# FF2 as seven products of quadrants, in a transformer layer on one core

## The chip, the cores and the metric

The kernel runs on one core of a Trainium2 chip. The time is the device time of one execution in microseconds; a run gives one time, and the median of several runs stands for a kernel. The profiled execution is one more run, with the hardware profiler on; its trace has every instruction.

Engines are called as in the profile: PE multiplies matrices (PEld loads its stationary operand), DVE and ACT work on tiles element by element, POOL does so too and issues DMAs, SP only issues DMAs.

## The reference

One layer: a token mixer (attention with a window, and a gated delta rule), a projection w_out, a layer norm, and an MLP with squared ReLU and a second norm. Sequence 1024, width 1024, hidden width 4096, float32. The part that the change touches is the end:

```python
mixed = (sigmoid(g_a) * y_a + sigmoid(g_b) * y_b) @ w_out
x = layer_norm(ALPHA * x + (1.0 + gt1) * mixed, ln1_g, ln1_b)
u2 = x * (1.0 + sc2) + sh2
h = square(relu(u2 @ w_ff1 + b_ff1))                              # FF1
x = layer_norm(ALPHA * x + (1.0 + gt2) * (h @ w_ff2 + b_ff2), ln2_g, ln2_b)   # FF2
```

## The kernel before

**Splits.** Each float32 operand is taken as a sum of two parts. ACT copies it into the high part, DVE subtracts that from the operand and has the low part (`split_s`, L215 and L216; "hi" and "lo" below). A product is three matmuls: hi·hi, hi·lo, lo·hi. The moving side is 512 columns wide.

**Seven products.** w_out's input and FF1 go by Strassen's scheme in Winograd's form: operands are cut into quadrants, sums of quadrants are formed, and seven products of halves replace eight.

**The order.** PE, DVE and ACT run in an order written out by the program: `at(p, f)` puts the instructions of `f` at matmul number p, counted from the start, and a matmul of 512 columns is one slot of it. `E0`, `F0` and `G0` are the slots at which w_out, FF1 and FF2 begin. The queues of SP (DMA) and of POOL (arithmetic and DMA) are ordered by a scheduler, and each runs in its order.

**w_out** (L1485): 4 segments of 96 matmuls. A segment is one half of the columns (`q`) and four of the eight token tiles; four weights of a segment are loaded and split. `mix_done` adds the residual and, when both halves are there, normalises the tile; `u2_done` then transposes it on PE (L1408), ACT writes the pieces to `rawu` (L1411), and the quadrants and sums are split (u11, u21, u22 and the sums' `mh`, `ml`).

**FF1** (L1805): 1344 matmuls, 16 pairs of hidden blocks, 7 products of 12 for each. A pair holds blocks 2i and 2i+1; POOL forms the sums of its weights (`f_sums`, `f_sums2`), `f_alpha`, `f_beta`, `f_gamma`, `f_delta` split them. The first 5 pairs (`EARLY`) are interleaved, since the second half of the tokens comes later; the other 11, here called dense, follow one after the other, 84 slots each. The results, four blocks of a pair, are squared and stored to DRAM (`hid_d`).

**FF2** (L1873): 1536 matmuls in six chunks over the hidden width, of 2, 6, 6, 6, 6 and 6 blocks; the weights of a chunk stay, the hidden blocks are loaded tile by tile and split, and each chunk's result is added to `acc` from PSUM (L1834). The residual is added tile by tile in the last chunk but one (`residual`), and in the last each tile is normalised (`norm2`) while PE works on the next.

Of the kernel before, what the change touches and what calls it, by code (L numbers as in the profile page):

```python
# [34 lines left out]
def hybrid_layer_kernel(ctx: ExitStack, tc: tile.TileContext,  # L35
# [42 lines left out]
    r_d = dram.tile([NT, P, D], F32, name="r_d")  # L78
    gt_d = dram.tile([2, D], F32, name="gt_d")
    res_d = dram.tile([NT, P, D], F32, name="res_d")  # L80
    hid_d = dram.tile([NT, P, D_FF // P, P], F32, name="hid_d")
# [83 lines left out]
    wseq += [in_cols(w_ff1, 2 * i * P) for i in range(EARLY - 1)]  # L165
# [1191 lines left out]
    def open_pe():  # L1357
# [5 lines left out]
        gt1 = pe.tile([P, D], F32, name="gt1", bufs=1)  # L1363
# [11 lines left out]
    xqs, rs = {}, {}  # L1375

    def x_load(q, t):
        xq = xqs[q, t] = pe.tile([P, HALF], F32, tag="xq", name="xq", bufs=4)
        nc.sync.dma_start(out=xq, in_=x[t * P:(t + 1) * P, halves[q]])

    def mix_done(q, t, pt):
        if q == 0:
            rs[t] = pe.tile([P, D], F32, tag="r", name="r", bufs=4)
        r = rs[t]
        rq = r[:, halves[q]]
        V.tensor_tensor(out=rq, in0=pt, in1=gt1[:, halves[q]], op=ALU.mult)
        V.scalar_tensor_tensor(out=rq, in0=xqs.pop((q, t)), scalar=ALPHA, in1=rq, op0=ALU.mult, op1=ALU.add)
        V.bn_stats(out=parts[:, t, q, :], in_=rq)
        if q == 0:
            return  # L1390
# [82 lines left out]
    for s in range(4):  # L1473
        for t in range(4):
            p = E0 + SEG * s + 48 * (t // 2)
            at(max(E0 + 15, p - 40), x_load, s % 2, 4 * (s // 2) + t)
    wt, bank = [], 0

# [11 lines left out]
    for s in range(4):  # L1490
        base, q, t0 = E0 + SEG * s, s % 2, 4 * (s // 2)
        del wt[:]
        groups = [[[0, 1], [2, 3]], [[0, 1], [2, 3]], [[4], [5, 6, 7]], [[4], [5], [6], [7]]][s]
        free = [(0, 0, 60, 72), (0, 0, 60, 72), (0, 0, 42, 60), (0, 0, 78, 84)][s]
        for ts in groups:
# [5 lines left out]
            for c in range(4):  # L1501
                if len(wt) == c:
                    wt.append(stream_w(max(0, base + free[c] - count[0]), 1))
                for pt, t in zip(pts, ts):
                    mix_mm(pt, slice(t * P, (t + 1) * P), c)
            for pt, t in zip(pts, ts):
                at(max(count[0] + 1, E0 + 28), mix_done, q, t, pt)
                if q == 1:
                    at(count[0] + 1, u2_done, t, count[0] + (34 if len(ts) == 2 else 24))

    assert count[0] == F0
    pf = pf_pool = None
    WF, ring, fraw, tls = {}, [0], {}, {}

    def ring_tiles(shape):
        n = ring[0]
        ring[0] += 1
        if n % 6 < 4:  # L1520
            pool, th, tl, bufs = wp, "wh", "wl", 4
        elif n < 6:
            pool, th, tl, bufs = pf, "fh", "fl", 2
        else:
            pool, th, tl, bufs = big2, f"h{2 + n % 6}", f"l{2 + n % 6}", 1
        return (pool.tile(shape, F32R, tag=th, name="wfh", bufs=bufs), pool.tile(shape, F32R, tag=tl, name="wfl", bufs=bufs))

    def w_split(name, src):
        WF[name] = hi, lo = ring_tiles([P, KT, P])
        split_s(hi, lo, src, 5)  # L1530

    def f_raw(i, j):
        raw = wp.tile([P, KT, P], F32, tag="wr", name="fraw", bufs=2) if i == 0 or (i, j) == (EARLY - 1, 2) else \
            pf.tile([P, KT, P], F32, tag=("fh", "fl")[j], name="fraw")
        nc.sync.dma_start(out=raw, in_=in_cols(w_ff1, (2 * i + j % 2) * P)[0])
        fraw.setdefault(i, {})[j] = raw

    def f_load(i):

        for j in range(2):  # L1540
            f_raw(i, j)

    def f_sums(i, E):

        f1, f2 = fraw[i][0], fraw[i][1]
        X = fraw[i]["x"] = pf.tile([P, 4, P], F32, tag="x", name="x", bufs=1)
        sub(E, X, f1[:, 0:4, :], f2[:, 0:4, :])
        E.tensor_tensor(out=f2[:, 0:4, :], in0=f2[:, 0:4, :], in1=f2[:, 4:8, :], op=ALU.add)
# [7 lines left out]
    def f_alpha(i, j=0):  # L1556
        w_split((i, "a"), fraw[i][j])
# [12 lines left out]
    def open_pf():  # L1570
        nonlocal pf, pf_pool
        pe_pool.__exit__(None, None, None)
        pf_pool = tc.tile_pool(name="pf", bufs=2, side="right")
        pf = pf_pool.__enter__()

    def tile_of(i, c):
        t = tls[i, c] = pf.tile([P, HALF], F32, tag="t", name="t", bufs=6)
        return t

    def bias(i, c):  # L1580
        f = 2 * i + c // 2
        return bf1[:, f:f + 1]

# [4 lines left out]
    def out_block(i, c):  # L1588
        t = tls.pop((i, c))
        f, h = 2 * i + c // 2, c % 2  # L1590
        nc.sync.dma_start(out=hid_d[4 * h:4 * h + 4, :, f, :].rearrange("t p c -> p t c"), in_=t.rearrange("p (t c) -> p t c", t=4))

    def full(i, c, pt):
        t = tls[i, c]
        V.tensor_tensor(out=t, in0=t, in1=pt, op=ALU.add)
        if i < EARLY and c == 0:
            after(3, square, i, c)
            return
        V.scalar_tensor_tensor(out=t, in0=t, scalar=0.0, in1=t, op0=ALU.max, op1=ALU.mult)
        out_block(i, c)  # L1600

    def square(i, c):
# [3 lines left out]
        out_block(i, c)  # L1606

    def last_block(i, c, pt):
# [3 lines left out]
        out_block(i, c)  # L1612
# [11 lines left out]
    OPEN_PF = F0 + 46  # L1624
# [7 lines left out]
    at(OPEN_PF, open_pf)  # L1632
    ring[0] = EARLY - 1
    at(F0 + 15, f_raw, EARLY - 1, 2)
    at(OPEN_PF + 6, f_alpha, EARLY - 1, 2)
    at(F0 + 42, f_raw, 0, 1)
    at(OPEN_PF + 16, f_raw, 0, 0)
    at(F0 + 84, f_sums, 0, V)
    at(F0 + 85, f_sums2, 0, V)
    at(F0 + 96, f_gamma, 0)  # L1640
    at(F0 + 104, f_beta, 0)
    at(pos[0, 5] + 10, f_delta, 0)
    for i in range(1, NPAIR):
        if i < EARLY:
            b = pos[i, 5]
            E = V if i == 1 else G
            at(b - (47 if i == 1 else 70), f_load, i)
# [5 lines left out]
        else:  # L1653
            b = pos[i, 1]
            d = 36 if i == EARLY else 0
            at(b - 104, f_load, i)
            at(b - 84, f_alpha, i)
            at(b - 84 + d, f_sums, i, G)
            at(b - 76 + d, f_sums2, i, G)
            at(b - 58 + d, f_beta, i)  # L1660
            at(b - 38 + d, f_gamma, i)
            at(max(b - 22 + d, pos[i - 1, 7] + 13), f_delta, i)


    chunks = [(0, 2)] + [(2 + 6 * c, 6) for c in range(5)]
    NCH = len(chunks)
    starts = [G0 + 2 * NT * 3 * f for f, _ in chunks]
    W2, hid, acc, rows_, rr = {}, {}, [None] * NT, {}, {}
    p2f = p2f_pool = None

    def w2_tiles(f):

        if f < 2:
            return ring_tiles([P, D])
        g = (f - 2) % 6
        if (f - 2) // 6 % 2 == 0:
            at_ = (big2, f"h{g}"), (big2, f"l{g}")
        else:
            at_ = ((big, f"l{2 * g}"), (big, f"l{2 * g + 1}")) if g < 4 else ((big2, f"h{2 + g}"), (big2, f"l{2 + g}"))
        return [pool.tile([P, D], F32R, tag=tag, name="w2") for pool, tag in at_]  # L1680

    def w2_load(f, raw):
        W2[f, "raw"] = raw
        nc.sync.dma_start(out=raw, in_=w_ff2[f * P:(f + 1) * P, :])

    def w2_split(f):
        raw = W2[f, "raw"]
        if f >= chunks[-1][0]:

            V.tensor_tensor(out=raw, in0=raw, in1=rows_["gt2"], op=ALU.mult)  # L1690
        W2[f] = hi, lo = w2_tiles(f)
        split_s(hi, lo, raw, 5)

    def hid_load0(m, raw):

        hid["raw", m] = raw.rearrange("p (t f c) -> p t f c", t=4, f=2)
        nc.sync.dma_start(out=hid["raw", m], in_=hid_d[4 * m:4 * m + 4, :, 0:2, :].rearrange("t p f c -> p t f c"))

    def hid_split0(m):
        hi, lo = ring_tiles([P, 4, 2, P])  # L1700
        split_s(hi, lo, hid["raw", m], 5)
        for i in range(4):
            hid[0, 4 * m + i] = hi[:, i], lo[:, i]

    units = [(c, t) for c in range(1, NCH) for t in range(NT)]

    def hid_tile(kind, n, dtype):
        return big.tile([P, 6, P], dtype, tag=f"h{2 * kind + n % 2}", name="hid")

    def hid_load(n):  # L1710
        c, t = units[n]
        hid["raw", n] = hid_tile(0, n, F32)
        nc.sync.dma_start(out=hid["raw", n], in_=hid_d[t, :, chunks[c][0]:chunks[c][0] + 6, :])

    def hid_split(n):
        hid[units[n]] = hi, lo = hid_tile(1, n, F32R), hid_tile(2, n, F32R)
        split_s(hi, lo, hid.pop(("raw", n)), 5)

    def open_p2f():
        nonlocal p2f, p2f_pool  # L1720
        pf_pool.__exit__(None, None, None)
        p2f_pool = tc.tile_pool(name="p2f", bufs=2, side="right")
        p2f = p2f_pool.__enter__()

# [12 lines left out]
    def rr_tile(t):  # L1737
        rr[t] = big.tile([P, D], F32, tag=f"h{6 + t % 2}", name="rr")
        nc.sync.dma_start(out=rr[t], in_=res_d[SLOTS[t]])

    def res_sums(t, i):

# [3 lines left out]
        else:  # L1746
            V.tensor_tensor(out=r, in0=r, in1=rows_["B2"], op=ALU.add)
            nc.sync.dma_start(out=res_d[SLOTS[t]], in_=r)

    def residual(t, i):  # L1750
        if i == 0:
# [161 lines left out]
```

## Time and profile before

| | us |
|---|---|
| median of 3 runs | 1919.66 (1917.45 to 1919.95) |
| the profiled execution | 1921.89 |
| its span | 1920.2 |
| w_out, 1143.00 to 1246.15 | 103.15 |
| FF1, 1246.15 to 1560.98 | 314.83 |
| FF2, 1560.98 to the last matmul | 351.37 |
| tail | 7.85 |

The stages follow one another on PE, so each can be read on its own; what comes before w_out stays as it is. A row of a timeline gives the start, the duration, engine, line and operation, the tiles written and read, their shapes, and in brackets the idle time of the engine ahead of it with what ended it. A row of groups gives, behind the bar, the busy time and the mean duration in ns, then idle time. A row of waits gives the waiting instruction, what it waited for, the total, the number and the longest.

### The profile page before, as it was taken

The numbers are of one execution on the slowest core, as the hardware profiler recorded it, in microseconds if no ns is written. First come the engines' busy times: TensorE is split into PE (matmuls) and PEld (weight loads), VectorE is DVE, ScalarE is ACT, GpSimd is POOL, SyncE is SP. The second block draws the span as 40 slices with busy tenths as digits, with TensorE's granted clock in tenths as the row PEclk, the third lists the DMA queues.
The fourth block names the chain that finished last, engine by engine and source line by source line (L and its number), as shares of the span: only waits on it lengthen the run. The fifth ranks groups of instructions, "written<-read, shape, count | busy, mean of one in ns | idle before, by whom it ended". The sixth has DMA issues, their size and how long they took to land.

```text
span 1920.2 us, 25900 instructions
## 1 busy us (share of the span) xinstructions
PE 1867.6 (97%) x9323; PEld 1542.8 (80%) x9323; DVE 1223.5 (64%) x2347; ACT 882.3 (46%) x1985; POOL 353.4 (18%) x437
## 2 busy tenths in 40 slices
PE   7999999999999999999999999989999999999998
PEld 5977788788887878888888887768888878888887
DVE  7678598898855666666644447774545435444677
ACT  3689666666654445554634223563333342211110
POOL 7333223433331000000001100004323200000000
PEclk8999999999999999999999999999999999999999
DMA  9655632232258444554347445245434355444422
GB/s 255 180 186 199 208 91 82 62 95 79 68 198 218 146 137 145 155 154 139 111 132 257 146 132 199 100 133 158 121 110 115 109 174 197 152 143 143 135 95 82
DMA packets 255273, 275.56 MB, mean 144 GB/s; under 512 B 23477, under 2 KB 202630, under 8 KB 254890
## 3 DMA queue, kind: packets, MB, share of 16 engines
q1 hardware_dynamic: 233802, 199.05, 34.7%
q0 software_dynamic: 21344, 74.88, 11.8%
q8 instruction: 73, 1.20, 0.2%
q14 instruction: 54, 0.44, 0.1%
HBM read 194.44 MB, written 77.34 MB: 142 GB/s over the span
## 4 chain that ended last, share of the span: by engine, by line
PE 79%; DVE 7%; ACT 4%; DMA 3%; issue 2%; POOL 0%; SPq 0%; ACTq 0%; POOLq 0%; DVEq 0%
PE mm L248 31%; PE mm L1805 8%; PE a L1873 6%; PE mm L1873 6%; PE b L1873 6%; PE b L1805 4%; PE a L1805 2%; PE mm L1485 2%; PE c L909 2%; DVE wl L216 1%; PE a L1485 1%; PE mm L188 1%; PE mm L187 1%; PE mm L186 1%; PE a L1167 1%
## 5 line engine op out<-in xcount | busy, mean ns | idle before, releaser
L248 PE MATMUL mm<-uh,wl 128*128 128x512 f32 x800 | 332.0, 415 | 0.0
L248 PE MATMUL mm<-ul,wh 128*128 128x512 f32 x800 | 321.2, 402 | 0.0
L248 PE MATMUL mm<-uh,wh 128*128 128x512 f32 x800 | 318.0, 398 | 0.0
L248 PEld LDWEIGHTS mm<-ul,wh 128*128 128x128 f32 x800 | 151.0, 189 | 26.7 <-issue 0.2
L248 PEld LDWEIGHTS mm<-uh,wl 128*128 128x128 f32 x800 | 151.6, 189 | 23.0 <-issue 3.9
L248 PEld LDWEIGHTS mm<-uh,wh 128*128 128x128 f32 x800 | 151.6, 189 | 21.3 <-issue 0.2
L215 ACT ACTIVATE hid<-hid 128x768 fp32r<-128x768 f32 x40 | 33.8, 845 | 177.5 <-PE a L1873 60.1
L1873 PE MATMUL a<-w,hid 128*128 128x512 f32 x486 | 115.0, 390 | 0.3 <-DVE hid L216 0.3
L1873 PE MATMUL mm<-w,hid 128*128 128x512 f32 (+1 forms) x486 | 112.6, 385 | 0.0
L1873 PE MATMUL b<-w,hid 128*128 128x512 f32 (+1 forms) x486 | 112.6, 385 | 0.0
L1873 PEld LDWEIGHTS a<-w,hid 128*128 128x128 f32 x486 | 91.1, 188 | 19.8 <-DVE hid L216 0.7
L216 DVE TENSOR_TENSOR wl<-wr,wh 128x1024 fp32r<-128x1024 f32 x84 | 102.2, 1219 | 6.4 <-ACT wh L215 6.4
L1873 PEld LDWEIGHTS b<-w,hid 128*128 128x128 f32 x486 | 90.1, 188 | 18.3
L1873 PEld LDWEIGHTS mm<-w,hid 128*128 128x128 f32 x486 | 90.1, 188 | 18.2
L215 ACT ACTIVATE wh<-wr 128x1024 fp32r<-128x1024 f32 x84 | 88.1, 1049 | 19.8 <-PE c L1485 12.3
L216 DVE TENSOR_TENSOR wfl<-fraw,wfh 128x1024 fp32r<-128x1024 f32 x44 | 64.2, 1460 | 45.0 <-ACT wfh L215 44.9
L842 DVE CUSTOM_DVE_ANT_0 nscore<-a,amask,nsink 128x256 f32<-128x256 f32 (+1 forms) x128 | 54.6, 464 | 34.3 <-PE a L835 33.5
L853 POOL TENSOR_TENSOR sm<-sm 128x256 f32<-128x256 f32 x56 | 55.6, 994 | 98.6 <-ACT sm L849 65.8
L1169 ACT ACTIVATE vn<-a,brk 128x128 f32<-128x128 f32 x64 | 23.5, 367 | 108.2 <-PE a L1167 107.4
L849 ACT ACTIVATE sm<-nscore,stat 128x257 f32<-128x257 f32 (+1 forms) x128 | 62.1, 488 | 4.1 <-DVE stat L842 3.6
L894 POOL TENSOR_SCALAR_AFFINE_SELECT pl<-ph 128x512 fp32r<-128x512 f32 x56 | 44.0, 786 | 90.4 <-DVE ph L887 71.7
L737 DVE TENSOR_TENSOR M<-M,stt 128x62 f32<-128x62 f32 (+30 forms) x62 | 57.8, 933 | 1.5
(544 smaller groups left out, 4621.9 us busy)
## 6 DMA issues: line engine op xcount, KB each, us to landing
wr<-in_w_in_dram SPq DMA_DIRECT2D x60, 512.0 KB, 3.7
fraw<-in_w_ff_dram SPq DMA_DIRECT2D x33, 512.0 KB, 4.2
hid_d<-t SPq DMA_DIRECT2D x64, 256.0 KB, 2.3
w2raw<-in_w_ff_dram SPq DMA_DIRECT2D x32, 512.0 KB, 3.4
hid<-hid_d SPq DMA_DIRECT2D x40, 384.0 KB, 3.3
adaw<-in_w_ada_dram SPq DMA_DIRECT2D x41, 256.0 KB, 2.7
adaw<-in_w_ada_dram SPq DMA_DIRECT2D x16, 512.0 KB, 6.4
wr<-in_w_out_dram SPq DMA_DIRECT2D x16, 512.0 KB, 3.8
```

Of the source, the lines that this page charges most:

```text
L215: A.activation(out=hi, in_=src, func=AF.Copy)
L216: after(lag, lambda: V.tensor_tensor(out=lo, in0=src, in1=hi.bitcast(F32), op=ALU.subtract))
L248: T.matmul(ts[half], lhsT=w[:, k, :], rhs=xx[k][:, sl], start=k == 0 and m == 0, stop=k == KT - 1 and m == 2)
L737: V.tensor_tensor(out=M[:, 0:s, s + 1:64], in0=M[:, 0:s, s + 1:64], in1=steps.pop(s), op=ALU.add)
L842: V.tensor_tensor_reduce(out=ns[:, i, 1:1 + W], in0=sc[:, i * 2 * P:i * 2 * P + W], in1=amask[:, mo:mo + W], scale=-1.0, scalar=nsink[:, 2 ...
L849: A.activation(out=sm[:, i, 0:1 + W], in_=ns[:, i, 0:1 + W], func=AF.Exp, scale=-1.0, bias=st[:, i:i + 1], accum_out=st[:, 2 + i:3 + i])
L853: G.tensor_tensor(out=sm[:, :, 1 + P:1 + 2 * P], in0=sm[:, :, 1:1 + P], in1=sm[:, :, 1 + P:1 + 2 * P], op=ALU.add)
L894: G.affine_select(out=flat4(part), in_=flat4(full), pattern=[[0, 4], [1 if odd else -1, P]], compare_op=ALU.is_ge if odd else ALU.is_gt, f ...
L909: T.matmul(av[:, 0:256], lhsT=vt[:, b, :], rhs=p_[:, m, :], start=p_ is full and m == 0, stop=p_ is prods[-1][1] and m == 1)
L1485: T.matmul(pt, lhsT=m[k][:, tok], rhs=w[:, k % 2, :], start=k == 0 and w is wh and m is mh, stop=k == KT - 1 and m is ml)
L1805: T.matmul(pt, lhsT=a[:, k0 + k, :], rhs=b[k], start=begin and k == 0 and x_ == 0, stop=k == 3 and x_ == 2, skip_group_check=True)
L1873: T.matmul(pt, lhsT=a[:, j, :], rhs=b[:, lo:up], start=j == 0 and x_ == 0, stop=j == n - 1 and x_ == 2)
```

## The change

**FF2** becomes seven products too. The hidden activations are cut into quadrants, half of the tokens by half of the hidden width (16 blocks), and w_ff2 likewise. The products run in the order 1, 2, 6, 5, 7, 3, 4; each has 8 steps of 24 matmuls, 1344 in all. A step loads one hidden piece (128 x 2 x 512, from `hf_d`) and one weight piece (from w_ff2, or for the products 4 to 7 from `wt_d`) and splits both. Results of a chain of products stay in PSUM and are added on; `take` copies or adds them to `acc`. The last three steps of the last product (`LAST`) run token tile by token tile. Gates, residuals and norms of all tiles stand in and behind the last product (`gated`, `norm2`).

**FF1** pairs block i with i+16, so that a pair has one block of each half. It stores three of its blocks and the four sums of blocks that FF2 needs (`h_sums`, `h_sums2`, on DVE). For the first five pairs a block is loaded back once (`again`).

**Weight sums:** for each pair of rows of w_ff2, `t_load` loads two tiles (SP), `t_make` forms four sums on POOL and stores the tiles to `wt_d` from POOL's queue. Fifteen of the sixteen rounds are placed in FF1 and use the one pair of tiles h6 and l6.

**w_out** takes the column halves in the order 0, 1, 1, 0, so that the third segment uses the second's weights; twelve weights are loaded instead of sixteen. The tokens' x is loaded as whole rows, and tiles 4 and 5 are finished together.

```diff
+    hf_d = dram.tile([7, D_FF // (2 * P), P, HALF], F32, name="hf_d")
+    wt_d = dram.tile([D_FF // (2 * P), 2, P, D], F32, name="wt_d")
...
-    for q in (0, 1, 0, 1):
+    for q in (0, 1, 0):
...
-        groups = [[[0, 1], [2, 3]], [[0, 1], [2, 3]], [[4], [5, 6, 7]], [[4], [5], [6], [7]]][s]
+        groups = [[0, 1], [2, 3]] if s < 2 else [[4, 5], [6, 7]] if s == 2 else [[4, 5], [6], [7]]
...
+    def again(i):
+
+        nc.sync.dma_start(out=tile_of(i, 0), in_=hf_d[0, i])
+
+    def h_sums(i):
+
+        a11, a21, a22 = tls[i, 0], tls[i, 1], tls[i, 3]
+        sa = sums_[i] = big2.tile([P, 2, HALF], F32, tag="h7", name="sa")
+        sub(V, sa[:, 1], a11, a21)
+        add_(V, a21, a21, a22)
+        sub(V, sa[:, 0], a21, a11)
+        put(5, i, a21)
+        nc.sync.dma_start(out=hf_d[5:7, i].rearrange("m p c -> p m c"), in_=sa)
+
+    def h_sums2(i):
+
+        sb = big2.tile([P, 2, HALF], F32, tag="l7", name="sb")[:, 0]
+        sub(V, sb, tls[i, 2], sums_[i][:, 0])
+        put(3, i, sb)
...
+    def t_load(n):
+        if n < T_IN:
+            ts = [big2.tile([P, D], F32, tag=f"{c}6", name="wx") for c in "hl"]
...
+            nc.sync.dma_start(out=ts[j], in_=w_ff2[f * P:(f + 1) * P, :])
+
+    def t_make(n):
+        (b11, b12), (b21, b22) = [[t[:, h] for h in halves] for t in wpair[n]]
+        sub(G, b11, b12, b11)
+        sub(G, b12, b22, b12)
+        sub(G, b22, b22, b11)
+        sub(G, b21, b21, b22)
+        for j in range(2):
+            nc.gpsimd.dma_start(out=wt_d[n, j], in_=wpair[n][j])
+
+    T_IN, T_STEP = 15, 72
...
+    ORDER = (1, 2, 6, 5, 7, 3, 4)
...
+    def s_split(s, j):
+        hi, lo = stp[s, j] = [s_tile(w, F32R, "sp") for w in PARTS[s % 4][2 * j:2 * j + 2]]
+        split_s(hi, lo, stp["raw", s][j], 5)
...
+    LAST = 3
+    for s in range(7 * NS):
+        p = G0 + 24 * s
+        at((p15 + 14, p15 + 26, p15 + 62, p15 + 64)[s] if s < 4 else p - 96 - 28, s_load, s)
+        for j in range(2):
...
+            elif s > 7 * NS - LAST:
+                q = p - 60 + 10 * j
+            else:
+                q = p - 46 + 10 * j
+            at(q, s_split, s, j)
...
+    for t in range(4):
+        at(G0 + 3 * PS + 20 + 40 * t, gated, t, 0, HALF, 0)
+        at(G0 + 5 * PS + 20 + 40 * t, gated, 4 + t, HALF, D, 0)
+        at(G0 + 6 * PS + 14 + 26 * t, gated, t, HALF, D, 1)
+        at(G0 + 6 * PS + 20 + 26 * t, norm2, t, [(0, HALF), (HALF, D)], 2)
```

Three places show how instructions move.

ACT's queue at the end of w_out and the start of FF1. `wh` are hi's of weights, `st` is the root of a norm, `rawu` the transposed pieces of a token tile, u11h and u21h hi's of their quadrants. Before, tiles 4 and 5 come one after the other; these are the rows of the second, with two weights between:

```order
L1411 ACTIVATE rawu<-b,sh_118,sc_119 128x128
L1393 ACTIVATE st<-st,eps_ln 128x1
L1411 ACTIVATE rawu<-b,sh_118,sc_119 128x128 x3
L215 ACTIVATE wh<-wr 128x1024
L215 ACTIVATE u11h<-rawu 128x2x128 x2
L1411 ACTIVATE rawu<-b,sh_118,sc_119 128x128 x4
L215 ACTIVATE wh<-wr 128x1024
L215 ACTIVATE u21h<-rawu 128x2x128 x2
```

And now:

```order
L1410 ACTIVATE rawu<-b,sh_118,sc_119 128x128 x2
L215 ACTIVATE wh<-wr 128x1024
L1410 ACTIVATE rawu<-b,sh_118,sc_119 128x128 x6
L215 ACTIVATE u11h<-rawu 128x2x128 x4
L1410 ACTIVATE rawu<-b,sh_118,sc_119 128x128 x8
L215 ACTIVATE u21h<-rawu 128x2x128 x4
```

The hi's of a quadrant now stand behind eight pieces in one run, where they stood behind four.

POOL's queue in FF1, a part of it among the dense pairs; `x` and `fraw` are a pair's weight sums. Before, each pair had four operations and nothing stood between pairs:

```order
L1436 TENSOR_TENSOR x<-fraw 128x512
L1548 TENSOR_TENSOR fraw<-fraw 128x512
L1436 TENSOR_TENSOR fraw<-fraw 128x512 x2
L1436 TENSOR_TENSOR x<-fraw 128x512
L1548 TENSOR_TENSOR fraw<-fraw 128x512
```

Now rounds of `t_make` (`wx`, and the stores to `wt_d`) stand between and within them:

```order
L1435 TENSOR_TENSOR x<-fraw 128x512
L1543 TENSOR_TENSOR fraw<-fraw 128x512
L1435 TENSOR_TENSOR wx<-wx 128x512 x3
L1702 DMA wt_d<-wx 128x1024
L1435 TENSOR_TENSOR wx<-wx 128x512
L1702 DMA wt_d<-wx 128x1024
L1435 TENSOR_TENSOR fraw<-fraw 128x512 x2
L1435 TENSOR_TENSOR wx<-wx 128x512 x3
L1702 DMA wt_d<-wx 128x1024
L1435 TENSOR_TENSOR wx<-wx 128x512
L1702 DMA wt_d<-wx 128x1024
```

The sums of a pair are behind the rounds that the scheduler put ahead of them, and a round's first operation waits for its load.

DVE's queue near the end. `hid` and `sp` are lo's, `acc` the token tiles. Before, one lo stands between the tiles:

```order
L216 TENSOR_TENSOR hid<-hid 128x768
L1834 TENSOR_TENSOR acc_14373<-acc_14373,b 128x512
L1841 BN_STATS st<-acc_14373 128x6
L1834 TENSOR_TENSOR acc_14373<-acc_14373,mm 128x512
L1841 BN_STATS st<-acc_14373 128x6
L1845 BN_AGGR st<-st 128x2
L1849 RECIPROCAL st<-st 128x1
```

Now, for the third of the four tiles that are normalised within the last product:

```order
L216 TENSOR_TENSOR sp<-sraw,sp 128x1024 x3
L1783 TENSOR_TENSOR acc_14502<-acc_14502,gt_14509 128x512
L1784 TENSOR_TENSOR acc_14502<-acc_14502,rr 128x512
L1778 BN_STATS stats<-acc_14502 128x6
L1789 BN_AGGR stats<-stats 128x2
L216 TENSOR_TENSOR sp<-sraw,sp 128x1024
L1793 RECIPROCAL stats<-stats 128x1
L1796 SCALAR_TENSOR_TENSOR acc_14502<-acc_14502,stats,g_14517 128x512
L1798 SCALAR_TENSOR_TENSOR acc_14502<-acc_14502,stats,b_14519 128x512
L1796 SCALAR_TENSOR_TENSOR acc_14502<-acc_14502,stats,g_14517 128x512
L1798 SCALAR_TENSOR_TENSOR acc_14502<-acc_14502,stats,b_14519 128x512
L216 TENSOR_TENSOR sp<-sraw,sp 128x1024 x2
```

The lo's of the last steps stand between whole tiles of gate, residual and norm; before, residuals lay in an earlier chunk, and one lo of 768 columns went with each tile.

More of the change, by code (lines that the diff above doesn't have):

```diff
@@ L1686, in w2_split @@
[L1686 to L1717, printed above, removed]
+            at(b - (34 if i == EARLY else 82), f_alpha, i)
@@ L1775, in hybrid_layer_kernel, with stat, gated @@
[L1775 to L1781 removed]
+    stats = {}
+    def stat(t, lo, up, n):
+        V.bn_stats(out=stats["all"][:, t, 6 * n:6 * n + 6], in_=acc[t][:, lo:up])
+    def gated(t, lo, up, n, src=None):
+        a = acc[t][:, lo:up]
+        V.tensor_tensor(out=a, in0=a if src is None else src, in1=rows_["gt2"][:, lo:up], op=ALU.mult)
+        V.tensor_tensor(out=a, in0=a, in1=rr[t][:, lo:up], op=ALU.add)
+        stat(t, lo, up, n)
@@ new lines, in norm2, with rest @@
+    def norm2(t, cuts, n):
+        st, r = stats["all"][:, t], acc[t]
+        V.bn_aggr(out=st[:, 18:20], in_=st[:, 0:6 * n])
+        A.activation(out=st[:, 20:21], in_=st[:, 19:20], func=AF.Sqrt, bias=eps_ln)
+        def rest():
+            V.reciprocal(out=st[:, 21:22], in_=st[:, 20:21])
+            for lo, up in cuts:
+                sl = slice(lo, up)
+                V.scalar_tensor_tensor(out=r[:, sl], in0=r[:, sl], scalar=st[:, 18:19], in1=rows_["g2"][:, sl],
+                                       op0=ALU.subtract, op1=ALU.mult)
+                V.scalar_tensor_tensor(out=r[:, sl], in0=r[:, sl], scalar=st[:, 21:22], in1=rows_["b2"][:, sl],
+                                       op0=ALU.mult, op1=ALU.add)
+                nc.sync.dma_start(out=out[SLOTS[t] * P:(SLOTS[t] + 1) * P, sl], in_=r[:, sl])
+        after(3, rest)
@@ L1859, in hybrid_layer_kernel @@
[L1859 to L1880 removed]
+    chain = {}
```

352 lines of the change are left out of this document (163 added, 189 removed).

## The prediction

> **What bounds the kernel now.** I read the page's first part, then the busy time by stage, the chain of waits, the waits of PE, and the timelines at the two places where PE stands still.
>
> ```profile
> span 1920.2 us, 25900 instructions
> PE 1867.6 (97%) x9323; PEld 1542.8 (80%) x9323; DVE 1223.5 (64%) x2347; ACT 882.3 (46%) x1985; POOL 353.4 (18%) x437
> ```
>
> ```profile
> core 0: us, PE busy (x) PEld busy (x) DVE busy (x) ACT busy (x) POOL busy (x), PEclk, DMA share, GB/s
> 1143.00:1246.15 103.15, 97.14 (x438) 79.07 (x436) 73.63 (x126) 41.54 (x88) 4.68 (x8) 0.97 0.44 154
> 1246.15:1560.98 314.83, 309.21 (x1359) 254.09 (x1358) 165.84 (x203) 128.59 (x196) 77.07 (x57) 0.99 0.44 125
> 1560.98:1912.35 351.37, 349.33 (x1555) 288.94 (x1553) 203.91 (x249) 73.64 (x95) 3.19 (x6) 1.00 0.42 142
> 1912.35:1920.20 7.85, 0.00 (x1) 0.00 (x0) 4.41 (x10) 0.29 (x1) 0.00 (x0) 0.75 0.18 67
> ```
>
> The four stretches are w_out, FF1, FF2 and the tail after PE's last matmul. PE is busy for all but 6 us of the first two and 2 us of the third: the kernel is bound by the number of matmuls, so one removed is worth its own duration as long as everything else still comes in time. The chain of waits gives that duration.
>
> ```profile
> 1520.35 5.44 PE mm L1805 x24
> 1899.88 4.08 PE mm L1873 x18
> ```
>
> 24 matmuls in 5.44 us: one **slot** is 0.2267 us, in FF1 and FF2 alike. What PE waits for from w_out on is little:
>
> ```profile
> PE mm L1485 <- DVE wl L216: 5.9, 2, 3.1
> PE c L1805 <- ACT wfh L215: 4.3, 1, 4.3
> PE b L1408 <- DVE r L1397: 1.0, 1, 1.0
> PE b L1873 <- ACT acc L1832: 1.8, 1, 1.8
> PE a L1873 <- DVE hid L216: 0.3, 1, 0.3
> ```
>
> The sum below goes against the profiled execution (1921.89 us, its span 1920.2 and 1.69 around it); the median of the runs, 1919.66, is 2.2 lower.
>
> **FF2: fewer matmuls.** Six chunks made 1536 matmuls; seven products of 8 steps of 24 make 1344. 192 x 0.2267 = -43.5. The waits of 1.8 and 0.3 belong to code that goes: -2.1. The last tile in halves adds some 0.3. **-45.3.** In the six products before the last, each step asks for two splits of ACT and two of DVE in 5.44 us; the nearest rows are FF2's own weight splits:
>
> ```profile
> L215 ACT ACTIVATE w<-w2raw 128x1024 fp32r<-128x1024 f32 x30 | 31.6, 1052 | 37.3 <-DVE w2raw L1690 31.7 <-DMA w2raw<-in_w_ff_dram 5.5
> L216 DVE TENSOR_TENSOR w<-w2raw,w 128x1024 fp32r<-128x1024 f32 x30 | 36.6, 1221 | 21.0 <-ACT w L215 21.0
> w2raw<-in_w_ff_dram SPq DMA_DIRECT2D x28, 512.0 KB, 3.4
> ```
>
> 2.1 and 2.4 us of 5.44, with loads of 3.4 us issued 28 us ahead: I cost the streaming at nothing, hidden under the 24 matmuls. Without that cover each of 56 steps could cost about 1 us.
>
> **FF2: the last product and the tail.** Here the change gives back. All residuals and norms now stand in or behind the last product. The costs of one tile on DVE:
>
> ```profile
> L1834 DVE TENSOR_TENSOR acc<-acc,mm 128x512 f32<-128x512 f32 x26 | 17.8, 686 | 38.9 <-PE mm L1873 38.7
> 1896.57 0.69 DVE L1841 BATCH_NORM_STATS2 st<-acc 128x6 f32<-128x512 f32 x1
> 1898.00 0.73 DVE L1852 SCALAR_TENSOR_TENSOR acc<-acc,st,g 128x512 f32<-128x512 f32 x1
> 1900.89 0.95 DVE L216 TENSOR_TENSOR hid<-hid 128x768 fp32r<-128x768 f32 x1
> 1916.91 0.48 DVE L1854 SCALAR_TENSOR_TENSOR acc<-acc,st,b 128x256 f32<-128x256 f32 x1
> ```
>
> Multiply, add and statistics: 3 x 0.69 and the gaps, 2.12. From the end of the statistics to the first scaling (aggregate, ACT's root, reciprocal) 1898.00 - 1896.57 - 0.69 = 0.74. Four scalings, 1898.00 to 1900.89: 2.89. In all 5.75. Before its last three steps the last product has 5 x 24 = 120 slots, 27.2 us; in them DVE's queue has the four adds left of the sixth product (2.8), twelve lo's (12 x 1.22 = 14.6) and four whole tiles (23.0): **40.4 us**. The lo's of the last three steps stand between those tiles, and PE waits for them. Not all of the 13.2 us of excess shows, since the queue starts ahead of need; placing the rows one after the other gives PE waits of 2.1, 3.5 and 4.3, 9.8 in all. Then a tile arrives from PE each 18 slots (4.08) and needs 5.75: PE ends 27.2 + 9.8 + 16.3 = 53.3 after the product's start, but DVE ends at 27.2 + 9.8 + 4.1 + 4 x 5.75 + 0.9 (the halves) = 65.0, and the last output lands 2.8 later (the row of 1916.91 ends at 1917.39 of a span of 1920.2): 67.7. In before's terms the same stretch is 192 slots and the tail of 7.85: 51.4. **+16.3**; with nothing late for PE still +6.5, with the whole excess +20.
>
> **w_out.** The two waits of 5.9 go with the four reloads. Behind each, PE is slow as well:
>
> ```profile
> 1194.58 0.50 PE L1485 MATMUL mm<-wl,mh 128*128 128x512 f32 x1 [3.06 <-DVE wl L216]
> 1197.34 0.63 PE L1485 MATMUL mm<-wh,mh 128*128 128x512 f32 x1
> 1197.77 0.63 PE L1485 MATMUL mm<-wl,mh 128*128 128x512 f32 x1
> ```
>
> Matmuls start 0.43 apart instead of 0.23, for some 3 us: 1.6 to 2.0 lost per stall, 3.6 for both. That is -9.5 at most. Against it: the last weight of the fourth segment is released only by its use in the third, so its lo (1.06 on ACT, then 1.22) stands in DVE's queue among the residuals of two tiles; I give 1 to 3 us and half a slow stretch. **-6** (-9 to -2). The Trainium skill ("TensorE: Matmul & The Clock Gate", section "What's actually happening") has the clock halved after an idle window of about 3.4 us. By that figure a 3.06 us stall would cost only itself, and this term would be near -3; the row shows the half rate behind 3.06, so the measurement decides.
>
> **FF1: the start.** t4 and t5 now come together, and ACT works off root, twelve to sixteen transposed pieces and the hi's in one run before the first product can start:
>
> ```profile
> L1411 ACT ACTIVATE rawu<-b,sh,sc 128x128 f32<-128x128 f32 x32 | 12.5, 459 | 3.7 <-PE b L1408 3.7
> L215 ACT ACTIVATE u11h<-rawu 128x256 fp32r<-128x256 f32 x8 | 2.9, 410 | 0.0
> ```
>
> 8 x 0.459 + 4 x 0.41 = 5.3 us of it lie behind the norm; placed in order the first product waits about 2.9, the second 2.5, with 2 to 3 us of slow clock: 8. Before: 4.3, 1.2 for transposes, 1.9 slow: 7.4. **+0.6** (-7 to +6).
>
> **FF1: the added work of POOL and DVE.** Each pair gains four DVE sums, and beside the pairs run 15 rounds of weight sums: load 2 x 512 KB (SP), four POOL operations, two stores (POOL). All rounds use one pair of tiles. The rows:
>
> ```profile
> 1443.65 1.29 POOL L1436 TENSOR_TENSOR x<-fraw 128x512 f32<-128x512 f32 x1 [12.02 <-DVE wd L216]
> 1445.02 1.76 POOL L1548 TENSOR_TENSOR fraw<-fraw 128x512 f32<-128x512 f32 x1
> 1444.94 0.69 DVE L1599 SCALAR_TENSOR_TENSOR t<-t 128x512 f32<-128x512 f32 x1
> 1445.55 2.31 DVE L216 TENSOR_TENSOR wfl<-fraw,wfh 128x1024 fp32r<-128x1024 f32 x1
> 1453.77 1.22 DVE L216 TENSOR_TENSOR wfl<-fraw,wfh 128x1024 fp32r<-128x1024 f32 x1
> L1436 DVE TENSOR_TENSOR rawu<-rawu 128x512 f32<-128x512 f32 x8 | 5.3, 688 | 0.1
> fraw<-in_w_ff_dram SPq DMA_DIRECT2D x28, 512.0 KB, 4.2
> res_d<-r POOLq DMA_DIRECT2D x8, 512.0 KB, 3.0
> ```
>
> A lo of 1.22 takes 2.31 when POOL works beside it, and POOL's 1.29 becomes 1.76: operations of the two with SBUF operands **take turns**. From 1444.94 to the end of the lo, 1447.86, three operations of 0.69, 1.29 and 1.22 (3.20) took 2.92: 0.91 of their sum. So I count the turns against the time there is. The Trainium skill ("SBUF — State Buffer", section "SBUF: two separate sides") says the same in words, an exclusive lock for a whole instruction between a GpSimd operation and a DVE operation with two SBUF inputs; the trace agrees, with 2.31 beside 1.22.
>
> *Interleaved pairs.* From the first round to the third weight of pair 5 lie about 300 slots, 68 us. POOL's queue holds five rounds and the sums of pairs 2 to 5 there, 36 x 1.29 = 46.4; DVE 11 lo's (13.4) and 35 operations of half the size (five lo's, four weight sums, ten squares, sixteen sums) x 0.69 = 24.2. 84 us, by 0.91 still 76: 8 to 16 over. PE waits for the end of that queue, since the hi of pair 5 stands on ACT behind POOL's sums, and behind it everything ACT owes PE's banks. **+12** (0, if the turns are hidden by other idle time, to +20).
>
> *Dense pairs.* In POOL's order the sums of pair 12 stand behind round 14, so between the third weights of pair 5 and of pair 12 ten rounds must pass in 548 slots: 124 us, **12.4 a round**. A tile's round is three POOL operations, a store and a load. Quiet: 3 x 1.37 (from 1443.65 to 1445.02) + 3.0 + 3.4 + 0.6 for the issue = 11.1; with the load at FF1's 4.2 and the operations at 1.76: 13.4. At 13.4 it costs 10. The turns give the same: POOL 68 x 1.29 = 87.7, DVE per pair 3 x 1.22 + 7 x 0.69 = 8.5, seven pairs 59.5, times 0.91: 134 of 124. **+10** (0 to +20). With slow clock behind such stalls, +3: FF1 in all **+25.6**.
>
> **The sum.** 1921.9 - 45.3 + 16.3 - 6 + 25.6 = 1912.5; on the median's level **1910**.
>
> **The rivals.** *FF1 hides its new work* (rounds of 11 to 12 us, turns inside idle time): only +0.6 and +3 of clock remain, 1890.5, or 1888 on the median's level. For it speaks POOL's 77 us of 315 in FF1, against it the 2.31. *The end isn't late for PE* and FF1 is as forecast: +6.5 instead of +16.3, 1900. *Slower: the rounds pace FF1.* A dense pair moved 2 MB in its 84 slots (two weights, four blocks); now three sums and 1.17 rounds of 2 MB come on top: 5.1 MB in 19 us, 268 GB/s, as much as the busiest slices of the page:
>
> ```profile
> GB/s 255 180 186 199 208 91 82 62 95 79 68 198 218 146 137 145 155 154 139 111 132 257 146 132 199 100 133 158 121 110 115 109 174 197 152 143 143 135 95 82
> ```
>
> So store and load could both go to 4.2 or more, 3 x 1.76 + 4.2 x 2 + 0.6 = 14.3, and a fourth operation of 1.29 where the second tile's comes between: 15.5. Ten rounds then lie 31 over, FF1 costs 47, and the time is 1931. The point from which it decides: the rest gives -35 (-45.3 + 16.3 - 6), of which 15.6 are spent elsewhere in FF1, so 19.4 over ten rounds: a round of 14.3. *The change doesn't do what it says:* FF2's steps are paced by something else than PE, 1 us each: 56 more than forecast, 1966.
>
> **Chances.** Forecast 0.40, FF1 hidden 0.25, end not late 0.06, rounds pace 0.25, FF2 paced 0.04. A measurement tells about 0.2% from no change, 1915.8 to 1923.5 being "same". The forecast's own range (1897 to 1924) lies two thirds below it and a quarter within. Faster: 0.25 + 0.06 + 0.26 = 0.57; same 0.14; slower 0.29. The range leaves out the lower part of the hidden case and the worst of the paced one: 1884 to 1938.
>
> **What would show it.** In the trace after: 1344 matmuls of FF2 and PE busy about 305 us there; waits of PE for the lo's of the last three steps, about 10 us; 12 us or more from the last matmul to the end; no stall in w_out above 3 us; in FF1 new waits of PE for weights of pairs 5 to 12, and rounds 12 to 14 us apart. It is wrong if POOL's loads and stores are quicker or slower than the rows of before, or if a wait stands where I have none: in FF2's first six products.

## The result, and the profile after

The changed kernel takes 1935.76 us, the median of four runs (1930.79 to 1939.32), beside 1919.81 for the kernel before: a ratio of 1.0079, with an interval of 1.0052 to 1.0107. It is slower; the forecast was 1910, faster. The time lies close to the rival in which the rounds of weight sums pace FF1 (1931). A round, here and below, is `t_load` and `t_make` for one pair of rows.

The profiled execution took 1930.79, the lowest of the four. Its stages, in the columns of before (w_out, FF1, FF2 up to the last matmul, tail):

```profile
core 0: us, PE busy (x) PEld busy (x) DVE busy (x) ACT busy (x) POOL busy (x), PEclk, DMA share, GB/s
1138.90:1241.46 102.56, 97.14 (x437) 79.44 (x436) 70.08 (x122) 38.52 (x86) 4.90 (x8) 0.97 0.43 150
1241.46:1598.90 357.44, 325.67 (x1360) 261.41 (x1359) 242.85 (x253) 142.65 (x217) 190.39 (x153) 0.95 0.70 235
1598.90:1920.80 321.90, 310.86 (x1363) 256.93 (x1361) 212.91 (x233) 117.01 (x129) 8.29 (x6) 0.98 0.62 211
1920.80:1929.10 8.30, 0.04 (x1) 0.00 (x0) 4.49 (x9) 0.29 (x1) 0.00 (x0) 0.50 0.16 63
```

| | before | after | difference | forecast |
|---|---|---|---|---|
| w_out | 103.2 | 102.6 | -0.6 | -6 |
| FF1 | 314.8 | 357.4 | +42.6 | +25.6 |
| FF2 and tail | 359.2 | 330.2 | -29.0 | -29.0 |

w_out also began 4 us earlier than in the profiled run of before. In the executions shown here that start lies between 1138.9 and 1147.5 with the same code ahead of it, so this part is not the change's. FF2 gives what was worked out, to the tenth. Of the miss of 22.4 us in the stages, 17.0 are FF1's and 5.4 w_out's; but w_out's gain came in FF1's first matmuls instead (6.0 us, worked out further down), so what went wrong lies in the rest of FF1.

How late FF1 is and where can be read by counting its matmuls. The columns are PE's busy time and matmuls of FF1's line alone:

```profile
core 0: us, PE busy (x), PEclk, DMA share, GB/s
1241.46:1356.90 115.44, 106.81 (x446) 0.98 0.76 256
1356.90:1492.70 135.80, 115.60 (x454) 0.90 0.75 254
1492.70:1593.00 100.30, 97.07 (x420) 0.98 0.55 185
1593.00:1598.90 5.90, 5.60 (x24) 1.00 0.78 240
```

446 matmuls are worth 101.1 us at 0.2267 each and took 115.4: 14.3 late by then, of which the kernel before had 10. The next 454, in pairs 5 to 10, are worth 102.9 and took 135.8: **32.9 lost**. Of these PE stood still for 20.2 (135.8 less 115.6 busy); the other 12.7 are slower matmuls, at a granted clock of 0.90. The last round is through at 1500, and over the next 420 matmuls (95.2 worth) 5.1 are lost, most of it at FF1's end; the last 24 lose 0.5. The large loss stands where the rounds are, and ends with them.

PE's waits in FF1 name ACT:

```profile
PE b L1844 <- ACT t L1585: 20.6, 5, 6.1
PE mm L1844 <- ACT t L1585: 3.1, 4, 1.9
PE mm L1844 <- DVE wl L216: 3.0, 1, 3.0
```

L1585 frees a bank of PSUM. ACT works in its written order, and ahead of that instruction it stands at the hi of `f_gamma`, which needs the last of a pair's sums on POOL. The last and longest of these waits, ACT's and then POOL's timeline; it is for pair 11, and its round is the fourteenth (number 13, from 0) with the first operation of number 14:

```profile
1491.11 1.06 ACT L215 ACTIVATE wh<-fraw 128x1024 fp32r<-128x1024 f32 x1 [9.16 <-POOL fraw L1435]
1492.08 0.67 ACT L1585 ACTIVATE t<-b,cols 128x512 f32<-128x512 f32 x1
```

```profile
1480.59 1.30 POOL L1435 TENSOR_TENSOR x<-fraw 128x512 f32<-128x512 f32 x1
1481.84 1.30 POOL L1435 TENSOR_TENSOR wx<-wx 128x512 f32<-128x512 f32 x1
1483.09 1.28 POOL L1543 TENSOR_TENSOR fraw<-fraw 128x512 f32<-128x512 f32 x1
1484.31 0.57 POOL L1702 DMA_DIRECT2D wt_d<-wx  x1
1487.27 1.25 POOL L1435 TENSOR_TENSOR wx<-wx 128x512 f32<-128x512 f32 x1 [2.38 <-DMA wx<-in_w_ff_dram]
1488.49 2.59 POOL L1435 TENSOR_TENSOR fraw<-fraw 128x512 f32<-128x512 f32 x2
```

ACT waits 9.16 us for a pair's sums (`fraw`). On POOL these are interleaved with a round (`wx`), and the second half of the pair's sums stands behind an operation that waits for a load. So a transfer whose result FF2 loads more than 160 us later (the first load from `wt_d` starts at 1652.4) holds PE in FF1. The last store of each round shows the pace. That of round 13 is the row of 1484.31 above, that of round 4:

```profile
1342.36 0.57 POOL L1702 DMA_DIRECT2D wt_d<-wx  x1 [0.30 <-POOL wx L1435]
```

Nine rounds in 142.0 us: **15.8 us a round**. The forecast had 12.4 available and took 13.4; the rival took 15.5. The chain of waits has ten loads of rounds in that stretch, of 4.1 to 6.8 us; these are the first two and the last two:

```profile
1347.66 5.08 DMA wx<-in_w_ff_dram
1365.42 6.27 DMA wx<-in_w_ff_dram
...
1469.74 6.76 DMA wx<-in_w_ff_dram
1482.95 4.18 DMA wx<-in_w_ff_dram
```

### The profile page after: what moved, and what is told of

Same layout as the page of the kernel before. It is cut to its first block, busy times and chain, and to the rows that moved or that the text cites. A ratio compares the mean times of both kernels' runs of the same rounds, so it can differ in the third digit from the quotient of the medians.

```text
span 1929.1 us, 25990 instructions
## 1 busy us (share of the span) xinstructions
PE 1844.8 (96%) x9131; PEld 1517.5 (79%) x9131; DVE 1305.1 (68%) x2375; ACT 936.5 (49%) x2037; POOL 472.3 (24%) x533
## 4 chain that ended last, share of the span: by engine, by line
PE 66%; DVE 11%; DMA 8%; POOL 5%; ACT 3%; issue 3%; SPq 0%; POOLq 0%; DVEq 0%; ACTq 0%
PE mm L248 31%; PE mm L1885 5%; DMA wx<-in_w_ff_dram 4%; PE a L1885 3%; PE b L1885 3%; POOL wx L1435 3%; PE mm L1844 3%; PE c L1885 2%; PE mm L1498 2%; PE b L1844 2%; PE c L909 2%; DMA wt_d<-wx 1%; DVE wl L216 1%; PE mm L188 1%; PE mm L187 1%
## 5 line engine op out<-in xcount | busy, mean ns | idle before, releaser
L216 DVE TENSOR_TENSOR sp<-sraw,sp 128x1024 fp32r<-128x1024 f32 x112 | 134.7, 1238 | 93.7 <-ACT sp L215 93.7
L215 ACT ACTIVATE sp<-sraw 128x1024 fp32r<-128x1024 f32 x112 | 112.8, 1054 | 136.2 <-PE b L1885 68.0
L1885 PE MATMUL mm<-sp 128*128 128x512 f32 x528 | 141.0, 397 | 5.4 <-DVE sp L216 5.4
L1885 PEld LDWEIGHTS mm<-sp 128*128 128x128 f32 x528 | 101.2, 192 | 27.8 <-DVE sp L216 6.5
L1435 POOL TENSOR_TENSOR wx<-wx 128x512 f32<-128x512 f32 x64 | 95.0, 1484 | 108.0 <-DMA wx<-in_w_ff_dram 83.5
L216 DVE TENSOR_TENSOR wl<-fraw,wh 128x1024 fp32r<-128x1024 f32 x43 | 61.4, 1449 | 70.4 <-ACT wh L215 70.4
L215 ACT ACTIVATE wh<-wr 128x1024 fp32r<-128x1024 f32 x81 | 85.0, 1049 | 20.4 <-PE c L1498 12.3
L1885 PE MATMUL a<-sp 128*128 128x512 f32 x336 | 93.5, 389 | 0.0
L215 ACT ACTIVATE wh<-fraw 128x1024 fp32r<-128x1024 f32 x43 | 45.3, 1055 | 91.6 <-PE b L1844 40.2
L1885 PEld LDWEIGHTS a<-sp 128*128 128x128 f32 x336 | 63.1, 188 | 13.1
L1885 PE MATMUL b<-sp 128*128 128x512 f32 x288 | 73.1, 389 | 0.0
```

The source lines that it names most:

```text
L215: A.activation(out=hi, in_=src, func=AF.Copy)
L216: after(lag, lambda: V.tensor_tensor(out=lo, in0=src, in1=hi.bitcast(F32), op=ALU.subtract))
L1435: E.tensor_tensor(out=out, in0=a, in1=b, op=ALU.subtract)
L1885: T.matmul(bank[t][:, lo:up], lhsT=a[:, f, t * P:(t + 1) * P], rhs=b[:, f, lo:up], start=begin and s % NS == 0 and f == 0 and x_ == 0, sto ...
```

## The experiments

Two theories at first: **A**, the rounds are too slow on their two tiles and hold up POOL's queue; **B**, POOL and DVE take turns, and the hidden sums of DVE make that dear. Two more came with the runs: **D**, the rounds' transfers or work cost by their amount; **E**, the order of the in-order queues. Times are medians; the changed kernel's 1935.8 stands for no effect. A stage's time comes from one profiled execution each, and FF1 with the same instructions took 357.4 in one program and 361.8 in another (the one of **The end**), so differences in FF1 below some 4 us say nothing. The kernel before, taken again beside each group of runs, had medians from 1918.8 to 1921.4, so differences between medians are good to some 3 us.

**No rounds.** `at(p, t_load, n)` and `at(p + 24, t_make, n)` are gone, and products 4 to 7 read w_ff2.

> Leaves out the sums of w_ff2 altogether (no loads, no POOL operations, no stores; FF2's products 4 to 7 read pieces of w_ff2 of the same size instead), so the output lacks them. Theory A (the rounds of weight sums, one behind the other on one pair of tiles, hold up POOL's queue and with it the pairs' own sums): FF1 falls from 357 us to 318 to 325 us, and the time to 1895 to 1902 us. Theory B (turns between POOL and DVE, with the hidden sums of DVE the larger part, or the hidden stores): FF1 stays above 340 us and the time above 1915 us.

1892.1 us (0.9852 of before, 0.9837 to 0.9868). FF1 took 315.9. The rounds are the cause: 41.5 us of FF1, 44 of the time. The hidden sums, hidden stores and loads that remain cost little without them; what FF1 gained at its start (6.0) is lost again mostly at its end, where a wait of 4.4 for FF2's first loads stays. B in its strong form is out.

**Three tiles.**

```diff
-            ts = [big2.tile([P, D], F32, tag=f"{c}6", name="wx") for c in "hl"]
+            ts = [big2.tile([P, D], F32, tag=("h6", "l6", "l7")[(2 * n + j) % 3], name="wx") for j in range(2)]
...
-        sb = big2.tile([P, 2, HALF], F32, tag="l7", name="sb")[:, 0]
-        sub(V, sb, tls[i, 2], sums_[i][:, 0])
+        sb = sums_[i][:, 0]
+        sub(V, sb, tls[i, 2], sb)
...
-        at(pos[i, 4] + 20, h_sums2, i)
+        at(pos[i, 4] + 36, h_sums2, i)
```

> All work is kept, but the rounds go round three tiles instead of two (the third comes from forming the fourth hidden sum in place). Theory A (latency of load, sums and store on one tile): each tile has one and a half rounds of time, 18.6 us where a round of about 15 us is needed, FF1 falls to 325 to 335 us, the time to 1903 to 1913 us. Theory B (turns between POOL and DVE, or the DMA queues' throughput): no change, 1928 to 1938 us.

1939.8 us; FF1 367.0, with one wait of PE of 11.3 us. More room did not help. It isn't a clean test, though: the scheduler used the room to put three rounds and the first operation of a fourth ahead of pair 2's sums in POOL's queue, where two had stood. That pointed to the order.

**Rounds without arithmetic.** The four `sub(G, ...)` of `t_make` are left out.

> Keeps the loads and stores of all rounds but leaves out POOL's four operations, so the weight pieces stored are unsummed. Theory A: a round shrinks by about 5 us to 9 to 10 us, below the 12.4 that there are, FF1 falls to 318 to 328 us and the time to 1896 to 1906 us. Theory D (the transfers alone crowd the queues, so that the pairs' own loads and stores are late): FF1 stays above 340 us, the time above 1915 us.

1921.4 us; FF1 345.9. Between the theories: 14 us below the changed kernel, but 29 above no rounds, though POOL computes nothing for them. What it still does is wait, in its waits of FF1:

```profile
POOL wt_d L1698 <- DMA wx<-in_w_ff_dram: 99.6, 23, 7.6
POOL x L1435 <- DVE wd L216: 47.5, 6, 9.1
```

The store stands in POOL's queue until the load is there: 99.6 us of POOL blocked, with the pairs' sums behind. Either that (E), or the transfers as such (D).

**No hidden sums.** DVE's four operations of `h_sums` and `h_sums2` are left out, the stores remain.

> Leaves out DVE's four hidden sums of each pair (64 operations of 0.69 us, 44 us of DVE and its turns with POOL); seven pieces are still stored, three of them unsummed, so the output lacks the sums. Theory B (turns between POOL and DVE hold up the rounds): FF1 falls by 15 us or more, the time to 1922 us or less. Theory E (queues): FF1 changes by less than 8 us, the time stays at 1928 to 1938 us.

1927.7 us (1926.6 to 1935.37, beside 1930.79 to 1939.32 of the changed kernel). In the profiled execution, one of the slower of its eight, neither FF1 nor FF2 is shorter: FF1 359.9 beside 357.4, FF2 and tail 330.0 beside 330.2. B, which asked for 15 us of FF1, falls. The 8 us between the medians are no more than the two spreads (as ratios to before 1.0028 to 1.0062, and 1.0052 to 1.0107); a smaller cost of the hidden sums, up to those 8 us, is not excluded.

**POOL by hand, in all stages**: the POOL engine is added to the engines that follow the written order; nothing else changes.

> Same operations, tiles and transfers; POOL too follows the written order, so that a round stands where its slot is (one each 72 slots, 16.3 us) and no longer ahead of the sums of pairs that are due earlier. Theory A in its narrower form (the rounds hurt because the scheduler put them ahead of the pairs' sums, not by their length): FF1 falls to 320 to 332 us, the time to 1898 to 1910 us. Theories B and D (turns, or transfers): no change, 1928 to 1938 us.

1927.2 us. FF1 fell to 334.1, but w_out began only at 1160.3, some 20 us later than in the changed kernel: the stages ahead lose by the written order. For FF1 the narrower theory was near, for the time it failed.

**SP and POOL by hand, from w_out on.**

> Same operations, tiles and transfers; from w_out on the queues of SP and POOL follow the written order too, so that a round's loads stand where their slot is and no longer wait at the head of SP's queue for the stores of the round before (89 us of waiting there in the changed kernel, 128 us with POOL alone by hand). Theory E (the cost is the in-order queues: a round placed early waits for its predecessor's store at the head of SP and POOL, and what the pairs need stands behind it): FF1 falls to 318 to 330 us, the time to 1896 to 1908 us. Theory D (the rounds' transfers and POOL operations cost by their mere amount): no better than POOL alone by hand, 1922 to 1930 us.

1921.6 us; FF1 344.9, worse than the 334.1 with POOL alone. The expectation failed. SP's waits in FF1:

```profile
SPq L1584 <- DVE t L1606: 65.0, 14, 7.0
SPq L1584 <- DVE t L1546: 51.9, 14, 5.9
SPq L1696 <- DMA wt_d<-wx: 43.7, 16, 8.2
```

The same three in the changed kernel:

```profile
SPq L1693 <- DMA wt_d<-wx: 89.4, 19, 11.1
SPq L1581 <- DVE t L1543: 44.7, 15, 9.1
SPq L1581 <- DVE t L1603: 28.2, 13, 7.2
```

The wait for a round's store fell by half, but in the written order stores of hidden blocks stand at the head of SP until DVE has them (117 us, where it was 73), and loads stand behind them. Beside the next run, which has the same written order of POOL and the scheduler's order of SP, this one is some 15 us slower: SP's order is a cost of its own, and the scheduler's was better. That these stores are the reason is read from the waits, not tried.

**POOL by hand, from w_out on.**

```diff
+    manual.__exit__(None, None, None)
+    manual = tc.manual_schedule(engines=order_all | {mybir.EngineType.Pool})
+    manual.__enter__()
     at(E0 + 15, open_pe)
```

> POOL follows the written order from w_out on only, so that the stages ahead keep theirs (with POOL by hand in all stages w_out began at 1160.3 instead of 1138.9, and FF1 took 334.1 us instead of 357.4). Theory E (order of the queue): FF1 again 330 to 338 us, w_out's start back at about 1142, the time 1905 to 1914 us. Rival: the gain in FF1 came from the shift of the earlier stages, and FF1 is back above 350 us, the time above 1925 us.

**1905.1 us** (0.9930 of before, 0.9902 to 0.9958). The same operations, tiles and transfers in another order, 31 us faster; FF1 took 323.1 instead of 357.4. The edit writes POOL's order alone, but the scheduler, which still orders SP, answered with another order there too: in the changed kernel the loads of round 1 are issued ahead of those of pair 3, here behind those of pair 5. What POOL waits for in FF1, in the changed kernel and then here:

```profile
POOL wx L1435 <- DMA wx<-in_w_ff_dram: 83.5, 26, 16.1
```

```profile
POOL wx L1435 <- DMA wx<-in_w_ff_dram: 22.1, 10, 4.5
```

And SP's wait ahead of a round's loads, here:

```profile
SPq L1696 <- DMA wt_d<-wx: 127.3, 26, 10.3
```

That is 38 us more than the 89.4 of the changed kernel, and FF1 is 34 us shorter all the same. This decides for E, the order of the queues; what of the 31 us is POOL's order and what the order of SP that came with it isn't separated. For D, the amount of the rounds' work, the 13 us remain by which this kernel stands above the one without rounds (1905.1 and 1892.1). FF1 alone shows 7 of them, since here the wait for FF2's first loads lies in FF2, not in FF1.

A large part of what remains stands at one place. From FF1's 121st matmul to its 505th 10.9 us are lost (without rounds 2.3), most of it here:

```profile
1348.89 0.69 DVE L1435 TENSOR_TENSOR sa<-t 128x512 f32<-128x512 f32 x1 [6.41 <-DMA t<-hf_d]
1352.83 0.80 PE L1847 MATMUL mm<-mh,wl 128*128 128x512 f32 x1 [4.71 <-DVE wl L216]
```

DVE stands at the hidden sums of the last interleaved pair until the block that is loaded back (`again`) has come, and the lo that PE waits for stands behind them. The same stall is in the two kernels below that keep this order. Moving it was not tried.

**Rounds in phase.** As the last, with `T_IN, T_STEP = 13, 84`, the first load 166 slots ahead of pair 5 instead of 180, and `t_make` 32 slots behind its loads.

> As f1, and thirteen rounds of 84 slots, one for each dense pair, each placed behind the pair's own two groups of sums, so that none stands between them (in f1 two rounds do, and PE stands still for 8.2 us behind one of them); three rounds in FF2. Theory E: FF1 316 to 326 us, the time 1892 to 1903 us. Theory D (amount): thirteen rounds instead of fifteen give 6 us at most, FF1 above 326.

1899.8 us (0.9905, 0.9873 to 0.9937), FF1 319.8. This is in the range of E, but 3.3 us of FF1 beside the kernel before it tell nothing more against D, and two rounds less stand in FF1. The stall of 8.2 us that the expectation puts behind a round stood at FF1's end in the run with POOL by hand in all stages; with POOL by hand from w_out on, PE's longest wait in FF1 is the 4.71 above, and here it is 5.5, at the same place.

**Eleven rounds.** `T_IN = 11` in the changed kernel, with the scheduler's order.

> Eleven of the sixteen rounds in FF1 instead of fifteen, the other five in FF2 on other tiles, where POOL and SP have room; a complete kernel. Theory A/E (each round beyond what fits costs what it is late): four rounds of about 15 us less in a stretch that is 32 to 43 us late: FF1 falls to 320 to 335 us, the time to 1898 to 1912 us. Theory F (only the start, with the interleaved pairs, is late, where all rounds up to the sixth stay): FF1 falls by less than 10 us, the time stays above 1924 us.

1916.9 us; FF1 343.1, between the two expectations: four rounds less are worth 14 us of FF1, 3.6 each and not 5.5 to 9. The version is a little better than the kernel before (0.9982, 0.9970 to 0.9995).

**The end.**

```diff
-                cuts = [0, HALF] if t < 3 else [0, HALF // 2, HALF]
+                cuts = [0, HALF]
...
-        at(G0 + 6 * PS + 14 + 26 * t, gated, t, HALF, D, 1)
-        at(G0 + 6 * PS + 20 + 26 * t, norm2, t, [(0, HALF), (HALF, D)], 2)
+        p = G0 + 6 * PS + (14, 40, 66, 124)[t]
+        at(p, gated, t, HALF, D, 1)
+        at(p + 1, norm2, t, [(0, HALF), (HALF, D)], 2)
```

> The last token tile is no longer cut in halves, and the norm of the fourth tile stands behind the lo's of the last three steps. Theory G (the end is set by DVE, and PE's waits there matter only where DVE then stands still: 2.6 us and 3.2 us): FF2 and tail together fall by 5 to 7 us, from 330 to 323 to 325. Theory H (PE's waits count in full): they fall by 11 to 14 us, to 316 to 319. Rival: no change, since DVE has the same work. FF1 as in the changed kernel.

FF2 and tail fell from 330.2 to 323.5, theory G. The lines of DVE that it speaks of, in the changed kernel:

```profile
1899.23 0.69 DVE L1783 TENSOR_TENSOR acc<-mm,gt 128x512 f32<-128x512 f32 x1 [2.59 <-PE mm L1885]
1920.87 0.42 DVE L1783 TENSOR_TENSOR acc<-c,gt 128x256 f32<-128x256 f32 x1 [3.17 <-PE c L1885]
```

and PE's waits there:

```profile
PE c L1885 <- DVE acc L1783: 5.7, 1, 5.7
PE mm L1885 <- DVE sp L216: 5.4, 2, 2.9
```

PE stood still for 11.1 us in the last product, but taking both causes away (0.4 of its waits is left) gave 6.7, about the two gaps of DVE (5.8) and the shorter operations that the halves cost. The end is set by DVE. FF1, which this edit leaves as it was in the changed kernel, took 361.8, and the time was 1932.2.

**Both ends.** Rounds in phase, the end above, and FF2's first splits 16 and 10 slots later.

> As f2, with the end of e6 (last tile whole, the fourth tile's norm behind the lo's) and the splits of FF2's first two steps 16 and 10 slots later, so that ACT does not wait for their loads ahead of what FF1's last pair needs (3.4 to 8.2 us of PE in the runs so far). By the runs: 6.7 us less than f2 for the end, 3 to 6 us for the splits: 1882 to 1894 us. Rival: the later splits make FF2's first steps late by as much as FF1's end gains, and only the end's 6.7 us remain.

**1895.8 us** (0.9885, 0.9855 to 0.9915), the best complete kernel here, though above the 1882 to 1894 expected. The rival on the splits fits: FF1 is 318.1, 1.7 less, but FF2's fourth step then waits:

```profile
PE mm L1889 <- ACT sp L215: 5.3, 1, 5.3
PE mm L1889 <- DVE sp L216: 1.7, 2, 1.3
```

FF2's first loads are slow with the scheduler's order and with POOL by hand: on the chains 10.4 us in the changed kernel, 12.1 with POOL by hand in all stages, 16.3 here. What differs is where PE waits for them. In the changed kernel and in the first two runs with POOL by hand it is FF1's last pair, and FF2 and tail took 330.2 us; in the two runs with POOL by hand from w_out on it is FF2, and FF2 and tail took 337.0 and 336.9. So FF1, FF2 and tail are better taken together: 687.6 for the changed kernel, 660.1 with POOL by hand from w_out on, 645.7 without rounds. Why the loads are slow was not tried.

## Why the prediction was wrong

- **FF2's matmuls (-45.3) and the last product with the tail (+16.3).** -29.0 in all, measured -29.0. The first six products were right: 1152 matmuls in 261.0, no wait among them. That the sum is right to the tenth is in part luck: the prediction's own rows give 67.7 for the last product and the tail, and they took 69.2; before had about as much more outside the rows that the sum counted. The bound, DVE, is right and is shown by the reordered end. The waits of PE were not: 9.8 was forecast for the lo's of the last steps and 5.4 came (2.5 and 2.9). Another, of 5.7, was not foreseen: it stands between the halves of the last tile, whose second half PE starts only when DVE has read the first from the same bank. So PE ended later, and the tail behind it was 8.3, not the 12 or more given as a sign.
- **w_out (-6) and FF1's start (+0.6).** Together -5.4. Measured -0.6 in w_out, but FF1's 121st matmul starts 29.3 us after its first where it was 35.3: -6.0, together -6.6. The wait of 4.3 in FF1 went, and in w_out one of 2.6 for the transposed pieces came. The sum was right, the split wrong. Behind a stall of 2.55 in w_out seven matmuls again start 0.43 apart, as the prediction read it; but not every stall has this, and behind the 3.43 at FF1's end (shown below) they start 0.23 apart.
- **Interleaved pairs (+12).** From the 121st matmul to the 446th the lateness grew by 12.2 us (2.1 to 14.3), by 2.0 before (8.1 to 10.1): +10.2. The size was right, and by luck, for the reason, turns of POOL and DVE, doesn't fit. Up to the start of the 447th matmul, the lateness grew by 12.3 in the changed kernel, without POOL's arithmetic for the rounds by 13.7, without the hidden sums by 10.1; with all the work in another order by 7.1, and without rounds by 1.7. The two do take turns, as the trace of before shows (a lo of 1.22 us took 2.31) and the Trainium skill says ("SBUF — State Buffer", section "SBUF: two separate sides"), but at 53% of POOL this was no bound.
- **Dense pairs (+10).** The step that failed: "At 13.4 it costs 10", and the sum took that 10 (and 3 for the clock). Dense pairs measured 32.9. The place and the mechanism were nearly right, a pair's sums behind the rounds in POOL's queue, though the last wait was for pair 11's, behind round 13 and an operation of round 14, and not for pair 12's. But a round took 15.8 and not 13.4: ten rounds at 15.8 beside the 12.4 available are 34, slower matmuls included, since PE goes at the rounds' pace. The round was priced as three operations, one store and one load (by its own rows 13.1), while the loads on the chain took 4.1 to 6.8, and beside them stood SP's 89 us of waits for the round before and the pair's sums between a round's operations. How much of the 15.8 each of these is was not measured apart. The rival had this size, 15.5 and +31, and the point of decision was 14.3.
- **Not in the sum: FF1's end.** PE waits 3.4 us more within the last pair, where ACT stands at the hi of FF2's first step until its load, 10 us on its way, has come (without rounds it waits 4.4 there, so this is not their doing):

```profile
1582.14 10.40 DMA sraw<-in_w_ff_dram
1592.57 0.68 ACT t L1585
1593.30 0.50 PE L1844 MATMUL b<-u22h,wh 128*128 128x512 f32 x1 [3.43 <-ACT t L1585]
```

- **"FF1 hides its new work"** had 0.25 and 1888. Most of the work can be hidden: 323.1 us of FF1 with all fifteen rounds. The order of the queues decided against it. The prediction took that order as given, as it had to, but weighed turns and round lengths where the places of the rounds were the larger matter.

## What to carry to other kernels

Work that is due late, on an in-order queue that also serves the critical path, must not stand ahead of what is due soon, however idle the engine looks: POOL was busy 53% of FF1, and the price of the order, with what it changed on SP, was 31 us. Price such a queue by the rounds that must pass before a given deadline, and take the loaded durations at the top of their range, since each wait adds to the next. Where a scheduler sets one queue and the program the others, look at where it puts the background work, and try the written order for that queue alone, from the stage where it matters. Look at the other queues then, too: a scheduler may answer there.

## What was not expected of the hardware

The amount that the DMA queues moved did not set the length of FF1. FF1 with the written order for POOL from w_out on:

```profile
1242.50:1565.60 323.10, 311.41 (x1359) 254.13 (x1358) 224.46 (x250) 142.15 (x216) 196.91 (x153) 0.99 0.74 253
```

253 GB/s at a busy share of 0.74 over the whole stage, with PE busy for 311 of 323 us at a clock of 0.99; the changed kernel moved 235 at 0.70 in 34 us more. But a load was dearer under that traffic: the median of a pair's weight load (`fraw`, 512 KB) was 4.2 us before, where FF1 moved 125 GB/s, and 5.4 in both of these kernels.
